# A third expert with a fixed place: three of its weight loads move ahead of the wait for the sorted experts

## The chip, the cores and the metric

One core of a Trainium2 chip runs the whole program as one launch. The metric is the device time in microseconds of that launch. The runs before the change took 867.78, 868.07 and 868.67 us; 868.07 is their median.

## The reference

Two residual layers on 256 tokens of width 1024, all in float32, then a last RMSNorm. Each layer is an attention mixer (layer 0: sparse attention beside block attention; layer 1: latent attention beside a sliding window) and then a mixture of experts. The change is in the mixture:

```
aff    = sigmoid(h @ router_w)                       # 256 x 16
g      = the group of 4 experts whose two best (aff + router_b) sum highest
expert = the 2 best experts of that group, w = aff of them / their sum
for each expert e, on the tokens that chose it:
    y = (silu(x @ w_gate[e]) * (x @ w_up[e])) @ w_down[e]
out[token] += w * y
```

There are 16 experts with `w_gate` and `w_up` of 1024 x 512 and `w_down` of 512 x 1024, 6 MB for one expert and 96 MB for a layer. All of them are read, whatever the router chooses; only the number of tokens on each differs.

## The kernel before

**Places and groups.** An expert's tokens are worked on in a *place*, a fixed number of 32-token blocks. `GROUPS` (L31) lists seven groups of places, four blocks (128 tokens) in each; a pair (p, n) is place p with n blocks. Which expert sits in which place is settled at run time: `places()` (L1357) ranks the first `SORTED` experts by their number of tokens, and place p gets the expert whose rank is `RANKS[p]`. The experts behind `SORTED` keep the place of their own number. Before, 14 experts are sorted, and experts 14 and 15 keep places 14 and 15, which are group 0. So group 0's weights can be requested before the router has run (`load_both`, L1179); all other groups need the sorted numbers, which VectorE writes into `ex_p` (L1378).

**A group** (class `Group`, L1211) does this: `__init__` reads the numbers of its experts from `ex_p` into registers of the engine that will request the weights (`load_value`, L1348, recorded at L1349). That engine is SP, for group 3 POOL. The read waits for `ex_p`, and everything behind it in that engine's queue waits too. `hidden` requests gate and up (`load_experts`, L1161, its requests at L1171): two tiles of 1 MB for each expert and matrix, h = 0 and 1 with four of the eight k rows each, all experts' first halves before the second halves. Then `gate_up` (L1096) runs the matmuls, one after the other over k, and in each k over the blocks (`parts`, from `blocks`, L1087: two blocks of 64 tokens for a group [2, 2], else four of 32). `rows` (L1272) requests the down weights if need be and runs the down matmuls; `combine` (L1140) adds the result to X.

**Order.** The loop at L1464 handles group i's `hidden`, then group i-1's `rows`, so the requests in SP's queue go: gate and up of group 0, then the wait for `ex_p`, gate and up of group 1, down of group 0, gate and up of group 2, down of group 1, and so on. Before group 3, SP requests group 2's down weights and comes to `rest()` (L1445). That is a chain of branches (L1453) for tokens that overflow their place: `rounds()` (L1386) has counted how many extra rounds of 64 tokens are needed, and none is run where nothing overflows. PE, ACT, DVE and SP take the branch; SP waits there for all its outstanding loads. POOL requests group 3's weights on its own queue and doesn't branch.

**Tiles.** Weights go through 15 tiles of 1 MB, 10 named `slot` and 5 named `room`, handed on as they are freed by the matmuls that read them (`slot`, L139). The same tiles carry the mixers' weights and the adaLN weights (`ada_load`, L250). Ahead of group 0 in a layer's expert stage stand two adaLN chunks, two tiles each.

The scheduler orders each engine's instructions by their place in the program and puts in the waits; SP's requests stand in its queue in the order in which they are written.

Of the kernel before, what the change touches and what calls it, by code (L numbers as in the profile page):

```python
# [17 lines left out]
ET = mybir.EngineType  # L18
# [4 lines left out]
NE, DE = 16, 512  # L23
# [4 lines left out]
RING, EXTRA = 10, 5  # L28


GROUPS = [[(14, 2), (15, 2)], [(0, 3), (1, 1)], [(2, 2), (3, 1), (4, 1)], [(5, 2), (6, 2)], [(7, 2), (8, 1), (9, 1)],  # L31
          [(10, 2), (11, 2)], [(12, 2), (13, 2)]]
RANKS = 0, 9, 1, 10, 11, 2, 3, 4, 12, 13, 5, 6, 7, 8
SORTED = len(RANKS)
BLOCK = 32


def shape_constants():
# [40 lines left out]
    iota = np.tile(1000 + np.arange(96, dtype=f)[None], (P, 1))  # L79
    ranks = np.tile(np.array(RANKS, f)[None], (P, 1))  # L80
    places = sorted(x for g in GROUPS for x in g)
    size = np.tile(np.array([BLOCK * n for _, n in places], f)[None], (P, 1))

    owner = np.concatenate([np.repeat(np.eye(len(g), dtype=f), [BLOCK * n for _, n in g], axis=0) for g in GROUPS], axis=1)
    rank = np.tile((4 - np.arange(4)).astype(f)[None], (P, 1))
# [22 lines left out]
def trunk(ctx, tc, ins, out):  # L108
    nc = tc.nc
    mm, vec, act, pool, sp = nc.tensor.matmul, nc.vector, nc.scalar, nc.gpsimd, nc.sync  # L110
# [14 lines left out]
    def bank(tag, shape, name=None):  # L125
        t = ps.tile([P, 512], F32, tag=tag, name=name or tag)
        n = 1
        for s in shape[1:]:
            n *= s
        v = t[:shape[0], :n]  # L130
        if len(shape) == 3:
            v = v.rearrange("p (a b) -> p a b", b=shape[2])
        elif len(shape) == 4:
            v = v.rearrange("p (a b c) -> p a b c", b=shape[2], c=shape[3])
        return v
# [3 lines left out]
    def slot(n_k, n):  # L139

        tag = order.pop(0)
        order.append(tag)
        t = room() if tag == "wx" else ring.tile([P, 2048], F32, tag="w", name="slot")
        return t[:, :n_k * n].rearrange("p (k f) -> p k f", k=n_k)

    def room():

        return rooms.tile([P, 2048], F32, tag="wx", name="room")
# [91 lines left out]
    def const(name):  # L240
        i, a, n = _WHERE[name]
        return KT[i][:, a:a + n]
# [7 lines left out]
    def ada_load(layer, n):  # L250
        return load_k8(ins["ada_w"][layer][:, n * 512:(n + 1) * 512])
# [69 lines left out]

    def ada_chunk(layer, c, W):


        v, half = divmod(c, 2)
        if half == 0 and v in (2, 5):
            GATE[v] = big.tile([P, D], F32, name="GATE", tag="GATE")
            pool.dma_start(GATE[v], ins["ada_b"][layer:layer + 1, v * D:(v + 1) * D].to_broadcast([P, D]))
        b = bank("tp", [P, 512])
        for k in range(8):  # L330
            g = (k % 4) * 32
            mm(b[g:g + 32], csil[:, k, 1 - half:33 - half], W[k], start=k < 4, stop=k >= 4)  # L332
            if k == 3:
                yield
        if half == 0:
            halves.append(ada_tile())
        t = halves[0]
        o, i = t, b
        if v not in (2, 5):
            o, i = t.rearrange("p (k m) -> p m k", k=8), b.rearrange("p (m k) -> p m k", k=8)  # L340
        if half == 0:
            act.copy(o, i)
            return
        vec.tensor_tensor(o, o, i, ALU.add)
        yield
        ada_end(layer, v, halves.pop())

    def fill(n=1):
        for _ in range(n):
            if fills:  # L350
                layer, c = fills.pop(0)
                W = first.pop(0) if first else ada_load(layer, c)
                for _ in ada_chunk(layer, c, W):
                    pass

    def ada_steps(n, rest):

        todo = [fills.pop(0) for _ in range(n)]
        W = ada_load(*todo[0])
        yield  # L360
        for i, at in enumerate(todo):
            ahead = ada_load(*todo[i + 1]) if i + 1 < n else None
            for _ in range(rest):
                yield
            yield from ada_chunk(*at, W)
            W = ahead
# [99 lines left out]
    def features(x, k=8):  # L466

        return x.rearrange("p (m k) -> p m k", k=k)

    def by_k(x, k=8):  # L470

        return x.rearrange("p (k m) -> p m k", k=k)
# [494 lines left out]
    def moe(cp, wk, layer, norm, end):  # L967
# [106 lines left out]
        def flush():  # L1074
            while late:
                late.pop(0)()

        def in_line():

            last = [None]  # L1080

            def add(*args, **kw):
                with tc.issue_after(last[0].ins) if last[0] else nullcontext():
                    last[0] = mm(*args, **kw)  # L1084
            return add

        def blocks(group):  # L1087


            ns = [n for _, n in group]  # L1090
            if ns == [2, 2]:
                return [(1, slice(64, 128)), (0, slice(0, 64))]
            at = [a for a, n in enumerate(ns) for _ in range(n)]
            return [(at[j], slice(BLOCK * j, BLOCK * j + BLOCK)) for j in reversed(range(4))]

        def gate_up(XG, c0, parts, Wg, Wu):  # L1096

            out = []
            for W, tag in ((Wg, "mm"), (Wu, "sc")):
                b = bank(tag, [P, 512])  # L1100
                put = in_line()
                for k in range(8):
                    for a, at in parts:
                        put(b[at], XG[:, k, c0 + at.start:c0 + at.stop], W[a][k], start=k == 0, stop=k == 7)
                out.append(b)
                flush()
            g, u = out
            hid = wk.tile([P, 512], F32, tag="hid", name="hid", bufs=1)
            hq = wk.tile([P, 512], F32, tag="hq", name="hq", bufs=1)
            act.activation(hid, g, AF.Silu)  # L1110
            vec.tensor_tensor(by_k(hq, 4), features(u, 4), features(hid, 4), ALU.mult)  # L1111
            return hq
# [66 lines left out]
        def load_both(nm, e0):  # L1179

            v = ins[nm][layer][e0:e0 + 2].rearrange("a (p k) f -> p a k f", k=8)
            tiles = []
            for k in range(0, 8, 2):
                t = slot(4, 512).rearrange("p (a k) f -> p a k f", a=2)
                sp.dma_start(t, v[:, :, k:k + 2, :])
                tiles.append(t)
            return [Rows([(t[:, a], 2) for t in tiles]) for a in range(2)]

        def pick_tile():
            return wk.tile([P, 2, 256], F32R, tag="pick", name="pick")  # L1190

        def picked(groups, pos):

            o = pick_tile()
            places, at = [x for g in groups for x in GROUPS[g]], 0
            while places:
# [9 lines left out]
        def gathered(o, n):  # L1206
            XG = hp.tile([P, 8, n], F32, tag="HT", name="XG")
            gather(XG, n, o)
            return o, XG

        class Group:  # L1211


            def __init__(self, i, o, XG, c0):
                self.first, self.last = i == 0, (layer, i) == (1, len(GROUPS) - 1)
                self.after = i == 3
                self.o, self.XG, self.c0 = o, XG, c0
                self.p0, self.n = GROUPS[i][0][0], len(GROUPS[i])
                self.parts = blocks(GROUPS[i])
                first = sum(len(g) for g in GROUPS[:i])  # L1220
                self.owner = const("owner")[:, first:first + self.n]
                es = list(range(self.p0, self.p0 + self.n))
                if i:
                    es = [load_value(ex_p[:, e:e + 1], [(ET.SP, ET.Pool)[self.after]], NE - 1) for e in es]
                self.es = es
                self.Wd = None

            def hidden(self):
                names = ("moe_w_gate", "moe_w_up")
                if self.first:  # L1230
                    W = [load_both(nm, self.p0) for nm in names]
                else:
                    W = [load_experts(nm, self.es, 8, queue=(sp, pool)[self.after], fine=self.last and nm == names[1])
                         for nm in names]
                self.hid = gate_up(self.XG, self.c0, self.parts, *W)

            def slots(self):
                self.OT = wk.tile([P, 2, P], F32R, tag="OT", name="OT")
# [109 lines left out]
        def load_value(at, engines, top):  # L1348
            _, v = nc.values_load_multi_w_load_instructions(  # L1349
                at, engines=engines, min_val=0, max_val=top, skip_runtime_bounds_check_because="sums of indicators")  # L1350
            return v[0]


        ex_p = cp.tile([1, 16], I32, name="ex_p")
# [103 lines left out]
        o, XG = gathered(*picked([0], route[:, 0:2]))  # L1458
# [5 lines left out]
        for i in range(len(GROUPS)):  # L1464
            p = Group(i, o, XG, 128 * (i > 0 and i % 2 == 0))
# [11 lines left out]
            if i % 2 == 0 and i < 5:  # L1477
                o, XG = gathered(*then)
# [299 lines left out]
```

## Time and profile before

| | |
|---|---|
| median of 3 runs | 868.07 us (867.78 to 868.67) |
| profiled execution | 869.42 us |
| its span, first to last instruction | 867.2 us |
| TensorE busy | 746.6 us, 86% of the span |
| VectorE, ScalarE, GpSimd busy | 377.8, 237.4, 115.6 us |
| mean granted TensorE clock | 0.932 |
| read from HBM | 289.16 MB, 335 GB/s over the span |

PE is TensorE's matmul row, DVE VectorE, ACT ScalarE, POOL GpSimd, SP the engine that issues most loads; a q behind a name (SPq, PEq) is the engine's sequencer, which waits, branches and issues. A busy share over the whole span is a mean over stages with different limits: the mixers of attention and the expert stages of the two layers have to be read apart.

### The profile page before, as it was taken

The numbers are of one execution on the slowest core, as the hardware profiler recorded it, in microseconds if no ns is written. First come the engines' busy times: TensorE is split into PE (matmuls) and PEld (weight loads), VectorE is DVE, ScalarE is ACT, GpSimd is POOL, SyncE is SP. The second block draws the span as 40 slices with busy tenths as digits, with TensorE's granted clock in tenths as the row PEclk, the third lists the DMA queues.
The fourth block names the chain that finished last, engine by engine and source line by source line (L and its number), as shares of the span: only waits on it lengthen the run. The fifth ranks groups of instructions, "written<-read, shape, count | busy, mean of one in ns | idle before, by whom it ended". The sixth has DMA issues, their size and how long they took to land. (4 is left out here: it accounts for less than half of the span.)

```text
span 867.2 us, 12251 instructions
## 1 busy us (share of the span) xinstructions
PE 746.6 (86%) x4499; PEld 381.9 (44%) x4499; DVE 377.8 (44%) x1091; ACT 237.4 (27%) x569; POOL 115.6 (13%) x118
## 2 busy tenths in 40 slices
PE   4699999999799969759997899979899967769996
PEld 1298765557443332214332568556443322214233
DVE  2285777767831231103206654876912031103214
ACT  1254545545311010001112454545111010002012
POOL 2020111233100001000011223344000001000001
PEclk9699999999699999879999999988699988979998
DMA  9999878796299998999999997733499989999992
GB/s 328 349 328 387 321 248 217 280 376 219 96 422 418 419 417 337 419 420 419 419 415 389 360 350 196 288 130 122 179 419 419 419 361 395 420 420 419 416 396 77
DMA packets 84840, 291.14 MB, mean 336 GB/s; under 512 B 9174, under 2 KB 23202, under 8 KB 63010
## 3 DMA queue, kind: packets, MB, share of 16 engines
q1 hardware_dynamic: 76976, 258.36, 77.9%
q0 software_dynamic: 4608, 29.37, 8.3%
q10 hardware_dynamic: 3186, 2.51, 0.9%
q8 instruction: 39, 0.64, 0.3%
q14 instruction: 31, 0.25, 0.1%
HBM read 289.16 MB, written 1.06 MB: 335 GB/s over the span
## 5 line engine op out<-in xcount | busy, mean ns | idle before, releaser
L1084 PE MATMUL o<-slot,hT 128*32 128x512 f32 (+2 forms) x448 | 93.5, 619 | 14.0 <-PEq L1453 13.1
L1084 PE MATMUL sc<-slot,XG 128*64 128x512 f32 (+1 forms) x416 | 92.1, 646 | 13.6 <-DMA slot<-in_moe_w_up_dram 13.6
L1111 DVE TENSOR_TENSOR hq<-sc,hid 128x512 f32<-128x512 f32 x14 | 14.7, 1049 | 184.3 <-PE sc L1084 184.3
L1084 PE MATMUL mm<-slot,XG 128*32 128x512 f32 (+1 forms) x416 | 85.9, 624 | 5.2 <-DMA slot<-in_moe_w_gate_dram 5.2
L507 ACT CAST hl<-slot 128x512 fp32r<-128x512 f32 (+2 forms) x112 | 60.7, 557 | 72.8 <-PE mm L524 45.8
L464 POOL TENSOR_TENSOR hl<-slot,hl 128x512 fp32r<-128x512 f32 x40 | 53.2, 1333 | 163.1 <-ACT hl L507 135.7
L1084 PE MATMUL mm<-room,XG 128*64 128x512 f32 (+1 forms) x224 | 57.1, 629 | 5.6 <-DMA room<-in_moe_w_gate_dram 5.6
L1084 PE MATMUL o<-room,hT 128*32 128x512 f32 (+2 forms) x208 | 58.6, 603 | 2.0 <-DMA room<-in_moe_w_down_dram 2.0
L1155 DVE SCALAR_TENSOR_TENSOR adac<-o,w,GATE 128x512 f32<-128x512 f32 (+1 forms) x29 | 21.2, 732 | 82.5 <-PE o L1084 81.5
L522 PE MATMUL mm<-HH,hl 128*128 128x256 f32 x176 | 54.5, 311 | 2.3 <-ACT HH L496 2.3
L1084 PEld LDWEIGHTS sc<-slot,XG 128*64 128x64 f32 (+1 forms) x416 | 25.3, 132 | 70.1 <-issue 48.6
L1137 ACT CAST yg<-adac 128x512 fp32r<-128x512 f32 (+1 forms) x28 | 17.1, 612 | 140.0 <-DVE adac L1155 140.0
L332 PE MATMUL tp<-slot,csil 128*32 128x512 f32 x344 | 49.2, 648 | 4.4 <-DMA slot<-in_ada_w_dram 4.2
L1084 PE MATMUL sc<-room,XG 128*32 128x512 f32 (+1 forms) x224 | 45.0, 656 | 8.3 <-DMA room<-in_moe_w_up_dram 8.3
L1068 ACT ACTIVATE XG<-tp,mod,mod 128x256 f32<-128x256 f32 (+1 forms) x32 | 17.2, 538 | 124.0 <-PE tp L1066 124.0
L524 PE MATMUL mm<-HH,hl 128*128 128x256 f32 x176 | 50.0, 286 | 0.6 <-DVE hl L464 0.6
L523 PE MATMUL mm<-HH,hl 128*128 128x256 f32 x176 | 50.4, 287 | 0.1
L1084 PEld LDWEIGHTS o<-slot,hT 128*32 128x32 f32 (+1 forms) x448 | 25.5, 125 | 54.3 <-issue 36.0
L464 DVE TENSOR_TENSOR hl<-slot,hl 128x512 fp32r<-128x512 f32 (+2 forms) x72 | 42.6, 611 | 15.3 <-ACT hl L507 15.0
L1066 PE MATMUL tp<-pick,XH 128*128 128x256 f32 (+1 forms) x128 | 41.9, 347 | 4.0 <-DVE XG L1070 2.6
L1145 DVE TENSOR_TENSOR X<-X,tp 128x512 f32<-128x512 f32 (+1 forms) x56 | 36.0, 675 | 16.5 <-PE tp L1144 16.2
L1144 PE MATMUL tp<-yg,OT 128*128 128x512 f32 (+1 forms) x112 | 36.6, 431 | 7.5 <-ACT yg L1137 3.5
(377 smaller groups left out, 1305.9 us busy)
## 6 DMA issues: line engine op xcount, KB each, us to landing
slot<-in_ada_w_dram SPq DMA_DIRECT2D x43, 1024.0 KB, 10.3
slot<-in_moe_w_gate_dram SPq DMA_DIRECT2D x37, 1024.0 KB, 15.1
slot<-in_moe_w_down_dram SPq DMA_DIRECT2D x35, 1024.0 KB, 19.7
slot<-in_moe_w_up_dram SPq DMA_DIRECT2D x34, 1024.0 KB, 18.6
room<-in_moe_w_up_dram SPq DMA_DIRECT2D x20, 1024.0 KB, 16.8
room<-in_moe_w_gate_dram SPq DMA_DIRECT2D x19, 1024.0 KB, 15.2
room<-in_moe_w_down_dram SPq DMA_DIRECT2D x17, 1024.0 KB, 18.8
slot<-in_ev_w_in_dram SPq DMA_DIRECT2D x8, 1024.0 KB, 9.5
```

Of the source, the lines that this page charges most:

```text
L332: mm(b[g:g + 32], csil[:, k, 1 - half:33 - half], W[k], start=k < 4, stop=k >= 4)
L464: eng.tensor_tensor(lo, v, hi.bitcast(F32), ALU.subtract)
L507: act.copy(hi, src)
L522: mm(o, a[0], b[0], start=start, stop=False, skip_group_check=True)
L523: mm(o, a[0], b[1], start=False, stop=False, skip_group_check=True)
L524: mm(o, a[1], b[0], start=False, stop=stop, skip_group_check=True)
L1066: mm(b, xk[i][:, t, k, :], o[:, t, 0:n], start=t == i == 0, stop=t == i == 1)
L1068: act.activation(XG[:, k, :], b, AF.Identity, bias=sh[:, k:k + 1], scale=fa[:, k:k + 1])
L1084: last[0] = mm(*args, **kw)
L1144: mm(cb, OT[:, t, :], x, start=i == 0, stop=i == 1)
L1145: vec.tensor_tensor(X[:, t, sl], X[:, t, sl], cb, ALU.add)
L1155: vec.scalar_tensor_tensor(v, y, w, gate[:, sl], ALU.mult, ALU.mult)
```

## The change

Three experts keep their place instead of two. Experts 14 and 15 stay in group 0; expert 13 keeps place 13 in group 1, beside the sorted place 12. The table of groups is written anew, so that group 1 is [2, 2] and group 3 is [3, 1]; `SORTED` falls from 14 to 13. In group 1 the blocks are taken in the other order, and the requests are made by a function of its own, `load_mixed`: both halves of expert 13's gate and the first half of its up, then the read of place 12's expert from `ex_p`, then that expert's gate, the second half of expert 13's up, and the sorted expert's up.

```diff
-GROUPS = [[(14, 2), (15, 2)], [(0, 3), (1, 1)], [(2, 2), (3, 1), (4, 1)], [(5, 2), (6, 2)], [(7, 2), (8, 1), (9, 1)],
-          [(10, 2), (11, 2)], [(12, 2), (13, 2)]]
-RANKS = 0, 9, 1, 10, 11, 2, 3, 4, 12, 13, 5, 6, 7, 8
+GROUPS = [[(14, 2), (15, 2)], [(12, 2), (13, 2)], [(0, 2), (1, 1), (2, 1)], [(3, 3), (4, 1)], [(5, 2), (6, 1), (7, 1)],
+          [(8, 2), (9, 2)], [(10, 2), (11, 2)]]
+RANKS = 1, 8, 9, 0, 10, 2, 11, 12, 3, 4, 5, 6, 7
...
-                if i:
+
+                self.mixed = i == 1
+                if self.mixed:
+                    self.parts = self.parts[::-1]
+                elif i:
                     es = [load_value(ex_p[:, e:e + 1], [(ET.SP, ET.Pool)[self.after]], NE - 1) for e in es]
...
                 if self.first:
                     W = [load_both(nm, self.p0) for nm in names]
+                elif self.mixed:
+                    W = self.load_mixed(*names)
...
+            def load_mixed(self, gate_, up):
+
+                e1 = self.es[1]
+
+                def half(nm, e, h):
+                    t = slot(4, 512)
+                    sp.dma_start(t, ins[nm][layer][bass.ds(e, 1)].rearrange("o (p k) f -> p (o k) f", k=8)[:, 4 * h:4 * h + 4, :])
+                    return t, 4
+                g1, u1 = [half(gate_, e1, 0), half(gate_, e1, 1)], [half(up, e1, 0)]
+                e0 = self.es[0] = load_value(ex_p[:, self.p0:self.p0 + 1], [ET.SP], NE - 1)
+                g0 = [half(gate_, e0, h) for h in range(2)]
+                u1.append(half(up, e1, 1))
+                u0 = [half(up, e0, h) for h in range(2)]
+                return [Rows(g0), Rows(g1)], [Rows(u0), Rows(u1)]
```

## Rows read from the trace of the kernel before

**Rows 1.** The page: GB/s that the DMA moved, in 40 equal slices.
```profile
GB/s 328 349 328 387 321 248 217 280 376 219 96 422 418 419 417 337 419 420 419 419 415 389 360 350 196 288 130 122 179 419 419 419 361 395 420 420 419 416 396 77
```

**Rows 2.** Stretches: us, busy PE, PEld, DVE, ACT, POOL, clock, DMA share, GB/s.
```profile
212.00:232.00 20.00, 14.44 (x89) 9.06 (x87) 14.89 (x58) 8.62 (x11) 6.23 (x2) 0.78 0.07 27
...
602.00:618.00 16.00, 12.13 (x61) 6.04 (x60) 12.90 (x48) 7.31 (x9) 5.95 (x2) 0.72 0.00 1
...
778.00:867.00 89.00, 77.08 (x398) 30.45 (x394) 28.06 (x52) 16.46 (x37) 3.89 (x4) 0.97 0.83 331
```

**Rows 3.** SP's waits (us, times, longest): 200:233, then 586:618, then 300:330.
```profile
SPq L1349 <- DVE ex_p L1378: 21.6, 1, 21.6
SPq L1349 <- PE mm L524: 6.9, 1, 6.9
...
SPq L1349 <- DVE ex_p L1378: 29.3, 1, 29.3
...
SPq L1453 <- SPq L1453: 27.0, 7, 5.3
```

**Rows 4.** Timeline of SP in layer 0: start us, us, request, count.
```profile
201.10 1.58 SPq L1185 DMA_DIRECT2D slot<-in_moe_w_up_dram  x2
231.94 1.91 SPq L1171 DMA_DIRECT2D slot<-in_moe_w_gate_dram  x3
234.09 0.41 SPq L1171 DMA_DIRECT2D room<-in_moe_w_gate_dram  x1
...
235.31 4.22 SPq L1171 DMA_DIRECT2D slot<-in_moe_w_up_dram  x3
...
262.57 3.82 SPq L1171 DMA_DIRECT2D slot<-in_moe_w_gate_dram  x3
...
300.85 0.33 SPq L1171 DMA_DIRECT2D room<-in_moe_w_down_dram  x1
329.38 7.72 SPq L1171 DMA_DIRECT2D room<-in_moe_w_gate_dram  x2
```

**Rows 5.** DMA 240:320, then the loads of 617.98, 251.99, 300.85: last, us to landing.
```profile
DMA packets 4597, 33.54 MB, mean 419 GB/s; under 512 B 507, under 2 KB 507, under 8 KB 507
...
slot<-in_moe_w_gate_dram SPq DMA_DIRECT2D x1, 1024.0 KB, 4.9
...
slot<-in_moe_w_gate_dram SPq DMA_DIRECT2D x1, 1024.0 KB, 21.2
...
room<-in_moe_w_down_dram SPq DMA_DIRECT2D x1, 1024.0 KB, 27.7
```

**Rows 6.** PE's waits (us, times, longest): 232:320, then 320:470, then 704:867.
```profile
PE o L1084 <- DMA room<-in_moe_w_down_dram: 0.9, 1, 0.9
...
PE sc L1084 <- DMA room<-in_moe_w_up_dram: 8.3, 1, 8.3
PE o L1084 <- PEq L1453: 6.8, 1, 6.8
PE mm L1084 <- DMA slot<-in_moe_w_gate_dram: 5.2, 1, 5.2
PE sc L1084 <- DMA slot<-in_moe_w_up_dram: 3.0, 2, 1.8
...
PE sc L1084 <- DMA slot<-in_moe_w_up_dram: 10.6, 3, 6.7
...
PE mm L1084 <- DMA room<-in_moe_w_gate_dram: 5.6, 2, 4.3
```

**Rows 7.** Timeline of PE: group 1's gate (second half) and up (both halves).
```profile
262.38 0.59 PE L1084 MATMUL mm<-room,XG 128*32 128x512 f32 x1
...
265.81 0.59 PE L1084 MATMUL sc<-slot,XG 128*32 128x512 f32 x1
...
269.24 3.62 PE L1084 MATMUL sc<-slot,XG 128*32 128x512 f32 x32
```

**Rows 8.** Timeline of DVE: the first of the sort's wide operations.
```profile
228.18 0.35 DVE L1369 TENSOR_TENSOR adac<-key 128x196 f32<-128x196 f32 x1
```

## The prediction, made before the changed kernel ran

> **What bounds the kernel now.** I read the page first, then the stretches around the two expert stages, then who waits there. The page's 40 slices of GB/s [rows 1] are what the reader is to see first: long runs at about 420, twice broken by a hole (the low values in the middle) in which attention and routing run, and then 420 again until the kernel is nearly over. 420 is the ceiling that this kernel reaches; the two expert stages live under it. The holes end in near-silence: from 212 to 232 us the DMA moves 27 GB/s, from 602 to 618 us 1 GB/s [rows 2]. SP's own waits say why [rows 3]: in layer 0 it waits 21.6 us, in layer 1 29.3 us, at L1349 for `ex_p` (L1378), the sorted experts. Every load of group 1 stands behind that read in SP's queue. SP's last load before the wait goes out at 201.10 (two of them, over by 202.68), the next at 231.94 [rows 4].
>
> Once the wait ends, loads follow one another at 419 GB/s [rows 5], 1,048,576 bytes in 2.50 us; that is the price of a 1 MB tile whenever the stream is full. The first one lands 4.9 us after its issue [rows 5], so 2.4 us of start-up come before 2.5 us of data; in a full stream the 2.4 us lie behind the load ahead.
>
> Two things stand in the way of simply saying "the stage is as long as its bytes". From 232 to 320 us TensorE waits for a load only once, 0.9 us [rows 6]: it is itself nearly full there, and data come well ahead (a load issued at 251.99 takes 21.2 us to land, so several stand in line [rows 5]). And at the branch of `rest()` (L1453) the queue drains. Behind the branch TensorE waits for loads 8.3 + 5.2 + 3.0 = 16.5 us in layer 0, and 10.6 + 5.6 = 16.2 us in layer 1 [rows 6]. So the load stream, not TensorE, decides when the stage ends, and TensorE has 16 us in hand in each layer.
>
> **The change part by part.**
> *Moved ahead of the wait:* expert 13's gate and up come in four loads of 1 MB; three of them (two of gate, one of up) now stand ahead of the read of `ex_p`. SP reaches them at 202.68. One wait that SP has there, 6.9 us for the last output-projection matmul [rows 3], may come before them: then they start at 209.6. Three loads: 2.4 + 7.5 = 9.9 us, landed by 219.5 at the latest. The wait ends at 231.94, so the silent stretch covers them with 12 us left; in layer 1 it is 29.3 us long. Cost 0; if the cover were gone they would cost their 7.5 us again, and nothing would be won. Nothing else is queued on SP behind them before the read of `ex_p`, and ACT's, POOL's and PE's queues are not touched. What they take off the stream behind the wait is 3 x 2.50 = 7.5 us per layer.
>
> *Buffers:* weights live in 15 tiles that are handed on as they come free. Four hold adaLN chunks, eight hold group 0; three are free. That is just what the early loads need: before, the first three behind the wait go out in 1.91 us, and the fourth at once too [rows 4]. But the hand-on order changes further down. Group 2's fourth to sixth gate loads take the next tiles that group 1 frees. Before, these were two gate tiles freed together as TensorE begins the second half of group 1's gate (262.38) and one more at 265.81 [rows 7]; SP's issue at 262.57 follows within 0.2 us [rows 4]. Now, in order of request, they are expert 13's gate tiles (free at 262.4 and 265.8) and its first up tile (269.24 [rows 7]). The load ahead of them lands at 251.99 + 21.2 = 273.2 before, 265.7 now. Fourth: issued 262.6, data could start at 265.0, no loss. Fifth: issued 266.0, data from 268.4 where the stream is free at 268.2, 0.2 lost. Sixth: 269.4, data from 271.8 against 270.9, 0.9 lost. So 1.1 of the 7.5 us go back: the lead is 6.4 us. TensorE wants these tiles only when groups 0 and 1 are through, and the 0.9 us are its one wait for a load up to 320 [rows 6]. Bounds of this term: 0 lost, or all three wait for group 1's last up tile at about 272.8: then the sixth lands at 272.9 + 2.4 + 7.5 = 282.8, later than before, and the lead is gone there. I take 1.1, since SP's issues follow TensorE's rows so closely.
>
> *The branch:* SP leaves it when its last load has landed, 300.85 + 27.7 = 328.55; the next goes out at 329.38 [rows 4, 5]. The drain is 27.0 us of waits, the jump's own 5.3 us (the longest of the seven) hidden under it [rows 3]. With a lead of 6.4 us SP leaves at 322.1. TensorE's stall of 6.8 us at the same branch [rows 6] hangs on no load, so it stays. Restart gap before: data again from 329.38 + 2.4 = 331.8, after 328.55: 3.2 us without data. I leave it as it is; it could shrink to 0 (POOL's loads for group 3 may still be in flight then), or grow by TensorE's 0.9.
>
> *Behind the branch:* POOL's last five loads of group 3 and SP's first of group 4 need only SP's exit, 6 x 2.5 = 15 us of stream; I take it as full as before, 6.4 us earlier. TensorE's 16.5 and 16.2 us of waits there are each more than that. What is late next is the same load stream. It carries to the end of the stage: in layer 0 the next layer's weights stand in the same queue, so layer 1 begins 6.4 us earlier as a whole; in layer 1 the last stretch is TensorE's (77.08 busy of 89 us [rows 2]), and it begins when the up weights of group 4 land.
>
> *Groups and sort:* 14 groups of matmuls before and after, as many of either shape (four groups with two blocks of 64, three with four of 32), so TensorE's work is the same. The sort goes over 13 instead of 14: five operations of about 0.35 us on 196 elements [rows 8] lead to `ex_p`, now on 169. At most 5 x 0.35 x 27/196 = 0.24 us per layer, at least 0; I take 0.1.
>
> *Overflow rounds:* counting the reference's router on its own inputs, no place overflows in either layer in either table (fullest expert 58 and 71 tokens on a place of 96; expert 13 has 26 and 23 on 64). So `rest()` runs nothing before or after.
>
> **The sum.** 2 x (7.5 - 1.1 + 0.1) = 13.0 us. Against the profiled execution's own time (869.42, with a span of 867.2) that gives 856.4; it lies 1.35 above the median of the runs shown, 868.07, so I forecast 855.1 for that.
>
> [...] The trace has 419 GB/s over 80 us [rows 5]. [...]
>
> **The rivals.**
> *Buffers in a worse order (lead halved).* If the scheduler hands the tiles on later than I worked out, 3 to 4 us per layer remain: 868.07 - 2 x 3.5 = 861. For: SP issues within 0.2 us of TensorE's release, so it does wait for buffers there. Against: loads in line cover 15 us and more.
> *TensorE is the bound (gain gone).* Only the 0.9 us in front of the branch is won: 868.07 - 2 x 0.9 = 866.3 or more. For: TensorE is nearly full from 232 on. Against: its 16 us of waits behind the branch.
> *A stall like the jump's.* At the branch TensorE stands 6.8 us that no load ends, with the DMA full [rows 6]. If the routing met one such stall per layer, because weights now move beside it, 6.8 - 6.5 would be left: 868.07 + 0.6, no change. Against: the three loads are over before the sort begins. [...]
> *Slower: the third early load finds no buffer.* It would stand in front of the read of `ex_p` until group 0's first gate tile is free, which is when SP's load of 239.2 goes out (the last of the three from 235.31 to 239.53 [rows 4]). The first load behind the wait would go out at about 240.2 instead of 231.94: 8.3 lost against 7.5 won and 1.1 lost again, 2 x 1.9: 871.9. It decides from the moment that fewer than three tiles are free. Against: four loads went out in 2.6 us behind the wait.
> *More: the restart gap closes too.* 2 x 3.2 on top: 848.7. For: POOL's loads run on beside SP's drain. Against: POOL's fourth waits for SP's exit too.
>
> **How the numbers follow.** Forecast 0.67 (851.5 to 858.5); halved lead 0.14; TensorE 0.05; stall 0.02; slower 0.05; gap closes 0.07. What the measurement can tell from no change is about 1.7 us (0.2%). Faster: 0.67 + 0.14 + 0.07 and a part of the TensorE case, 0.89. Slower 0.05, same 0.06. The range goes from 850, half of the last rival outside, to 862.5, which takes in most of the halved lead; outside lie about 0.18.
>
> **What would show it.** In the SP timeline three loads of expert weights before 215 us and before 605 us, and five instead of eight between the wait and group 0's down loads. GB/s in 212 to 232 up by at most 3 MB. SP's first load behind the branch near 323 instead of 329.4. TensorE's load waits behind the branch smaller by about 6 us per layer; both stages shorter by the same. I am wrong if the first load behind `ex_p` comes later than 1 us after the cast of `ex_p`, if the branch is left at 328 as before, or if TensorE's waits behind it shrink while the stage doesn't.

## The result, and the profile after

The changed kernel took 857.44 us (median of four runs, 857.31, 857.58, 859.34 and 854.84), the kernel before beside it 867.92: ratio 0.9876 [0.9849, 0.9903], 10.5 us less. The profiled run took 857.31 us with a span of 855.6; the rows below are from it.

The page's line for GB/s [rows 1]:
```profile
GB/s 326 347 321 385 325 274 201 260 400 294 136 423 364 419 419 339 419 421 418 419 418 391 357 363 185 262 203 270 116 419 381 418 346 412 420 418 419 416 398 89
```
The hole is shallower near its end in both layers (294 and 136 where 219 and 96 stood, 203 and 270 where 130 and 122 did). But two dents are new: 364 in slice 13 and 381 in slice 31, just where the stream before ran at 420.

Stretches of the changed kernel, columns as in [rows 2]; the last two are the 36 us around the *hand-on* of buffers, in which TensorE reads group 1's tiles for the last time and SP loads group 2's weights into them; they ran at 418 and 419 GB/s before:
```profile
212.00:232.00 20.00, 14.46 (x90) 9.09 (x89) 14.83 (x58) 8.62 (x11) 6.20 (x2) 0.80 0.38 156
602.00:618.00 16.00, 12.19 (x65) 7.18 (x59) 15.52 (x67) 3.89 (x8) 1.26 (x1) 0.82 0.25 92
...
246.00:282.00 36.00, 35.29 (x178) 15.03 (x173) 6.96 (x19) 4.68 (x10) 0.00 (x0) 1.00 0.96 387
628.00:664.00 36.00, 35.29 (x180) 15.34 (x176) 8.24 (x22) 5.91 (x11) 0.00 (x0) 1.00 0.99 396
```
The silent stretch of layer 0 carries 2.6 MB more (20 us x 129 GB/s). A full stream has 420, so 387 over 36 us are 36 x 33/420 = 2.8 us without data, and 396 are 2.1 us. In layer 0 all of it lies where group 2's fourth to sixth gate load are asked for:
```profile
262.00:276.00 14.00, 14.00 (x68) 4.86 (x68) 1.06 (x1) 1.16 (x2) 0.00 (x0) 1.00 0.88 336
```
14 us at 336 GB/s are 2.8 us without data. That is what the hand-on took back.

SP's timeline in layer 0 [rows 4]:
```profile
203.21 0.99 SPq L1249 DMA_DIRECT2D slot<-in_moe_w_gate_dram  x2
206.58 0.33 SPq L1249 DMA_DIRECT2D slot<-in_moe_w_up_dram  x1
232.29 0.96 SPq L1249 DMA_DIRECT2D room<-in_moe_w_gate_dram  x2
...
264.10 6.36 SPq L1171 DMA_DIRECT2D slot<-in_moe_w_gate_dram  x3
...
324.61 12.51 SPq L1171 DMA_DIRECT2D room<-in_moe_w_gate_dram  x2
```
Three loads go out ahead of the read. Group 2's fourth to sixth gate load (264.10, 267.5, 270.1) go out later than before (262.6, 263.1, 266.1), and behind the branch SP starts 4.8 us earlier (329.38 before; the branch, L1453 before, is L1474 now).

PE's waits [rows 6], 320:470 and then 704:856:
```profile
PE sc L1084 <- DMA room<-in_moe_w_up_dram: 9.7, 1, 9.7
PE o L1084 <- PEq L1474: 5.2, 1, 5.2
PE mm L1084 <- DMA slot<-in_moe_w_gate_dram: 3.1, 2, 2.8
...
PE sc L1084 <- DMA slot<-in_moe_w_up_dram: 1.6, 1, 1.6
PE o L1084 <- DMA room<-in_moe_w_down_dram: 1.0, 1, 1.0
...
PE sc L1084 <- DMA slot<-in_moe_w_up_dram: 9.9, 2, 8.5
PE mm L1084 <- DMA room<-in_moe_w_gate_dram: 5.4, 1, 5.4
```
The waits for loads behind the branch add up to 15.4 us in layer 0 and 15.3 in layer 1. The 15.4 hold a wait of 1.0 us for a down load; before, there was such a wait too, and the prediction's 16.5 leave it out:
```profile
PE o L1084 <- DMA room<-in_moe_w_down_dram: 1.1, 1, 1.1
```
Like for like, then, 17.6 us became 15.4 in layer 0 and 16.2 became 15.3 in layer 1: 2.2 and 0.9 us less, and yet the kernel is 10.5 us faster.

### The profile page after: what moved, and what is told of

Read it like the earlier page. It is cut to its first block, busy times and chain, and to the rows that moved or that the text cites. A ratio compares the mean times of both kernels' runs of the same rounds, so it can differ in the third digit from the quotient of the medians.

```text
span 855.6 us, 12225 instructions
## 1 busy us (share of the span) xinstructions
PE 745.3 (87%) x4499; PEld 384.6 (45%) x4499; DVE 377.7 (44%) x1095; ACT 237.3 (28%) x569; POOL 114.5 (13%) x118
## 5 line engine op out<-in xcount | busy, mean ns | idle before, releaser
L1084 PE MATMUL o<-slot,hT 128*32 128x512 f32 (+2 forms) x464 | 96.3, 621 | 8.7 <-PEq L1474 8.7
L1084 PE MATMUL sc<-slot,XG 128*32 128x512 f32 (+1 forms) x464 | 91.9, 612 | 11.5 <-DMA slot<-in_moe_w_up_dram 11.5
L1084 PE MATMUL mm<-room,XG 128*32 128x512 f32 (+1 forms) x288 | 65.8, 612 | 5.4 <-DMA room<-in_moe_w_gate_dram 5.4
L1084 PE MATMUL o<-room,hT 128*64 128x512 f32 (+2 forms) x192 | 59.7, 598 | 1.0 <-DMA room<-in_moe_w_down_dram 1.0
L1084 PEld LDWEIGHTS sc<-slot,XG 128*32 128x32 f32 (+1 forms) x464 | 26.6, 125 | 61.2 <-issue 47.8
L1084 PE MATMUL sc<-room,XG 128*32 128x512 f32 (+1 forms) x176 | 39.7, 647 | 9.7 <-DMA room<-in_moe_w_up_dram 9.7
## 6 DMA issues: line engine op xcount, KB each, us to landing
slot<-in_moe_w_down_dram SPq DMA_DIRECT2D x35, 1024.0 KB, 15.3
```

## The experiments

**The same instructions again, and TensorE's blocks turned round.** The first run repeats the changed kernel. The second takes its block order back:
```
 if self.mixed:
-    self.parts = self.parts[::-1]
+    pass
```


> The changed kernel again, as the level for the runs beside it. All theories: 857.4 us, between 854.8 and 859.3 as its first four runs lay, some 10.5 us under the kernel before.

> TensorE reads expert 13's block ahead of expert 12's in group 1, where the changed kernel reads them the other way round. Theory (the hand-on loses 2.7 and 1.9 us a layer since expert 13's buffers, first in the line, come free late): they come free about 1 us earlier, the 4th load behind them starts near 263 instead of 264.1 us in the first layer, and about 1 us a layer comes back: 855.4 us. Rival (TensorE waits for expert 12's tiles either way, so that both blocks end together): 857.4 us, unchanged. Other side: the two blocks' out-of-step order shifts to the up weights and costs as much there, 858 to 859 us.

Measured: 854.93 us, ratio 0.9854 [0.9835, 0.9873], and 856.24 us, 0.9873 [0.9855, 0.9890] (before: 867.49). The blocks' order makes no difference in the time that can be told; the streams through the hand-on are 394 and 386 GB/s in the one, 397 and 395 in the other, 5.1 and 4.1 us without data. So the order is not the main cause of the loss. It has a small part in it: with the blocks turned back, group 2's fourth load goes out 7.09 us after TensorE begins group 1's gate (254.94 to 262.03), in the changed kernel 7.95 us after (256.15 to 264.10); the sixth goes out some 14 us after in both.

**Two misses: loads moved in the text alone.** The requests were written behind the read of `ex_p`, all three in one kernel, the up load in the other:
```
-g1, u1 = [half(gate_, e1, 0), half(gate_, e1, 1)], [half(up, e1, 0)]
 e0 = self.es[0] = load_value(ex_p[:, self.p0:self.p0 + 1], [ET.SP], NE - 1)
+g1, u1 = [half(gate_, e1, 0), half(gate_, e1, 1)], [half(up, e1, 0)]
```


> The new grouping and the new order of the loads stay, but all three loads of expert 13 stand behind the read of the sorted experts. Theory (the whole gain is the three loads' early start): their lead of 7.5 us a layer is gone and with it the loss at the hand-on of buffers, so the time of the kernel before, 868 us, within 1.5 us. Rival (the new grouping helps by itself, by its narrower sort, by the order of TensorE's two blocks or by another order of buffers): part of the 10.5 us stays, 862 to 865 us.

> Only the two gate loads of expert 13 are requested ahead of the read; the up load stands behind it. Theory (the third load's lead is spent where buffers are handed on, since expert 13's first gate buffer comes free at 264 us in the first layer and no earlier): the lead is 5.0 us a layer, the buffers are then needed 2.5 us later than with three and little is lost at them (0.2 us where three lost 2.7 us), so 4.8 and 5.0 us a layer are left where three leave 4.7 and about 5.9: 858 us, within 1 us of the changed kernel. Rival (the gain goes by the bytes requested early): two thirds of 10.5 us, so 861 us.

Measured: 854.97 and 855.47 us, ratios 0.9858 [0.9833, 0.9883] and 0.9851 [0.9831, 0.9871]. Taken at its word the first would have refuted the theory. Its SP timeline says otherwise:
```profile
203.21 0.99 SPq L1249 DMA_DIRECT2D slot<-in_moe_w_gate_dram  x2
206.80 0.33 SPq L1249 DMA_DIRECT2D slot<-in_moe_w_up_dram  x1
231.91 0.95 SPq L1249 DMA_DIRECT2D room<-in_moe_w_gate_dram  x2
```
The loads still stand ahead of the read: the scheduler has put requests that could go in front of a read that couldn't yet. In both kernels SP's requests come in the changed kernel's order, and the traces hold as many instructions, so both count as the changed kernel once more. (The statement ahead of the prediction, that SP's requests stand in its queue as they are written, is thus not true of requests written behind a read that waits.) What they give is a measure of scatter: one program, four medians of 854.9 to 857.4 us. Differences under some 2.5 us aren't told apart here.

**None, one, two and four loads ahead.** Now an order on SP's instructions holds the loads (none ahead; the others likewise); for four, the second up half goes ahead too:
```
+read, (e0,) = nc.values_load_multi_w_load_instructions(ex_p[...], engines=[ET.SP], ...)
+with tc.issue_after(read[0].ins): g1, u1 = [half(gate_, e1, 0), half(gate_, e1, 1)], [half(up, e1, 0)]
```


> All three loads of expert 13 are held behind the read of the sorted experts, by an order put on SP's instructions; all else is as in the changed kernel (855.1 us in the last round of runs, the mean of three runs of the same instructions; the kernel before 867.5). Theory (the gain is the early start of the three loads, less what the hand-on takes back): 867.5 us, 866 to 869. Rival (the new grouping alone helps): 862 to 865 us.

> One load of expert 13, its first gate half, ahead of the read, two behind. Theory (each 1 MB load ahead gives a lead of 2.5 us a layer, as long as the hand-on of buffers takes none of it back, which it did to 1.9 to 2.7 us of 7.5 with three): 2.5 us in each of two layers, 862.5 us. Rival (by bytes, a third of 12.4 us): 863.4 us. The two agree here; what would speak against both is a step (867 or 856 us).

> Both gate loads of expert 13 ahead of the read, the up load behind it, now held there by an order on SP's instructions. Theory (the third load's lead is spent where buffers are handed on): 5.0 us in each layer with 0.2 us lost, so 858 us at most; against three ahead the third load is then worth 2 to 3 us at most over both layers. Rival (by bytes, two thirds of 12.4 us): 859.3 us.

> A fourth load ahead of the read: the second up half of expert 13 too, into a buffer of the other pool. Theory (buffers handed on by TensorE at group 1 already hold back group 2's loads with three ahead): the fourth lead is lost there in whole, 855 us, within 1 us of three ahead. Rival (by bytes, each load ahead 2.5 us a layer, as long as its buffer is free): 850 us. Other side: its buffer isn't free before the read, so that SP waits for it with the sorted loads queued behind: 856 to 862 us.

Measured (before: 867.96): 867.30, ratio 0.9994 [0.9975, 1.0013]; 862.94, 0.9938 [0.9917, 0.9958]; 857.31, 0.9871 [0.9851, 0.9892]; 857.19, 0.9877 [0.9857, 0.9897]. Without the early start the change is worth nothing that can be measured: grouping, sort and block order together bring 0.7 us. The first load ahead brings 4.4 us and the second 5.6, about the 2 x 2.5 us that each is priced at. The third and the fourth bring nothing beyond the scatter. The fourth found its buffer, at 218.26, long before the read. The same two stretches, none ahead, then two, then four:
```profile
246.00:282.00 36.00, 34.56 (x174) 15.29 (x170) 8.04 (x22) 5.90 (x11) 0.00 (x0) 1.00 1.01 419
628.00:664.00 36.00, 35.28 (x174) 14.52 (x170) 6.15 (x17) 4.40 (x8) 0.00 (x0) 1.00 1.01 420
```
```profile
246.00:282.00 36.00, 35.01 (x176) 15.07 (x172) 7.66 (x21) 4.98 (x10) 0.00 (x0) 1.00 1.00 409
628.00:664.00 36.00, 35.29 (x178) 15.21 (x174) 7.17 (x19) 4.67 (x9) 0.00 (x0) 1.00 1.00 413
```
```profile
246.00:282.00 36.00, 34.56 (x174) 15.15 (x171) 7.70 (x21) 5.91 (x11) 0.00 (x0) 1.00 0.96 387
628.00:664.00 36.00, 35.30 (x180) 15.02 (x176) 10.28 (x25) 5.91 (x11) 0.00 (x0) 1.00 0.92 370
```
TensorE's busy time hardly moves (34.6 to 35.3 of 36 us), the stream's rate does. With none ahead SP asks for group 2's fourth load at 262.08, 31.0 us after the first load behind the read; with two at 263.38, 32.0 after; in the changed kernel 31.8 after. Counted from the moment at which TensorE begins group 1's gate (254.14, 255.47, 256.15) it is 7.91 to 7.95 us in all three. The buffers come free when TensorE gets there, whatever lies ahead of the read; each load ahead only shortens the line of loads that hides that.

**TensorE made busier ahead of the hand-on.** Group 0's up gets ten matmuls more:
```
-for k in range(8):
+for n, k in enumerate([*range(extra), *range(8)]):   # extra = 5 for group 0's up, else 0
```


> The changed kernel, with ten matmuls more (five of the eight k rows of group 0's up weights are multiplied a first time, and their sums are then overwritten): 5 pairs of 0.43 us, 2.2 us more of TensorE in each layer, ahead of group 1's gate. Theory (with three loads ahead it is TensorE's own work up to group 1's gate that sets when buffers come free for group 2's fourth to sixth load, so the lead is spent there to the last us): 2.2 us a layer lost, 4.3 us, so about 861 us, 7 us under the kernel before instead of 11. Rival (what holds the loads there is the stream itself or the wait for the sorted experts, and TensorE has room): unchanged, 857 us, 11 us under before.

Measured: 866.71 us, ratio 0.9981 [0.9967, 0.9995]; 1.4 us under before (868.07) instead of 11. The direction is the theory's; its size was wrong, since a pair of these matmuls takes 0.86 us and not 0.43. TensorE's timeline of group 0's up:
```profile
242.97 3.60 PE L1084 MATMUL sc<-room,XG 128*64 128x512 f32 x16
246.41 1.02 PE L1084 MATMUL sc<-slot,XG 128*64 128x512 f32 x4
247.27 3.60 PE L1084 MATMUL sc<-room,XG 128*64 128x512 f32 x16
```
From 242.97 to 247.27 the five extra pairs took 4.30 us, not 2.2: 8.6 us over two layers, 9 to 11 were lost. In the two stretches the stream fell to 348 and 322 GB/s, 6.2 and 8.4 us without data. So TensorE's work there is paid in full once the loads are ahead. What the same ten matmuls would cost the kernel before was not run. An estimate from its rows: its fourth load went out at 262.57 and the load ahead of it landed at 273.2, so the load could go out 8.2 us later (up to 273.2 - 2.4) without a gap in the stream, and 4.3 us would cost the stream nothing. In layer 1 the trace of this run also has some of TensorE's matmuls in another order than the changed kernel, from group 1 to behind the branch, so the excess over 8.6 us, up to 2.6, isn't explained.

**Group 0's down weights ahead instead, and its rows too.** Group 0's experts are known, so its down weights could always have gone ahead of the read. On the kernel before:
```
 p.hidden()
+if i == 0: p.load_down()          # both kernels
 if before is not None:
     before.rows()                 # second kernel: for i == 1 ahead of p.hidden()
```


> The kernel before, its grouping kept (two experts in place), with one edit: the four down loads of group 0, whose experts are known, are requested ahead of the read of the sorted experts instead of behind group 1's gate and up. Theory: the lead is the same as with four loads of expert 13 (10 us at most), but the buffers of these loads are given back only when TensorE has multiplied group 0's down, part of it behind group 1's gate and up, so group 2's loads wait longer: more than half of the lead is lost, 860 to 866 us. Rival (the lead counts by its bytes, whichever weights it holds): 848 to 852 us.

> As the run with group 0's down loads ahead, and TensorE multiplies group 0's down ahead of group 1's gate. Theory (the hand-on by TensorE is what spends the lead): the four buffers come free near 262 to 264 us instead of one each at 263.5, 266.9 and 269.6 us, so less of the lead is lost: 5.5 to 7.5 us a layer are left of 10, so 853 to 857 us, at or below the changed kernel. Rival (the lead is capped elsewhere, near 5.3 us a layer, whatever is ahead): 857 us. Other side: group 1's gate comes 3.6 us later on TensorE, and the loads that take its buffers wait for that: 860 us.

Measured (before: 868.07): 866.43, ratio 0.9984 [0.9969, 0.9999]; and 852.67, 0.9821 [0.9799, 0.9842], below both kernels. These four loads ahead alone win almost nothing; with group 0's down multiplied ahead of group 1's gate, so that TensorE gives their buffers back early, they pay. (That order of TensorE's without the loads ahead was not run. In the kernel before the stream is full through this stretch, at 418 and 419 GB/s, so it has no gap there to close.) SP's timeline and TensorE's of the second:
```profile
202.82 3.82 SPq L1171 DMA_DIRECT2D slot<-in_moe_w_down_dram  x3
217.59 0.33 SPq L1171 DMA_DIRECT2D room<-in_moe_w_down_dram  x1
231.32 0.35 SPq L1171 DMA_DIRECT2D room<-in_moe_w_gate_dram  x1
...
261.60 3.78 SPq L1171 DMA_DIRECT2D slot<-in_moe_w_gate_dram  x3
```
```profile
254.04 1.08 PE L1084 MATMUL o<-slot,hT 128*64 128x512 f32 x4
...
264.94 0.62 PE L1084 MATMUL mm<-slot,XG 128*32 128x512 f32 x1
```
Group 0's down runs from 254.04, group 1's gate only at 264.94. The fourth to sixth load of group 2 go out within 3.8 us from 261.60, where the changed kernel takes 6.4 us from 264.10:
```profile
246.00:282.00 36.00, 35.28 (x240) 14.33 (x236) 9.98 (x20) 5.05 (x9) 0.00 (x0) 1.00 0.99 404
628.00:664.00 36.00, 35.29 (x252) 14.42 (x252) 10.70 (x22) 6.01 (x11) 0.00 (x0) 1.00 0.98 400
```
The kernels so far in one table. Lead: 2 layers x 2.5 us x loads ahead. Lost: 36 x (420 - GB/s)/420 over the two stretches. Measured: median of before less that of the kernel.

```
loads ahead                GB/s       lead   lost   left   measured
none                       419, 420    0      0.1   -0.1    0.7
one                        419, 420    5.0    0.1    4.9    5.0
two                        409, 413   10.0    1.5    8.5   10.7
three (the change)         387, 396   15.0    4.9   10.1   10.5
three, again               394, 386   15.0    5.1    9.9   12.6
three, blocks turned back  397, 395   15.0    4.1   10.9   11.3
four                       387, 370   20.0    7.1   12.9   10.8
three, TensorE busier      348, 322   15.0   14.6    0.4    1.4
down of group 0            320, 338   20.0   15.6    4.4    1.6
down and rows of group 0   404, 400   20.0    3.1   16.9   15.4
```
The two misses, the changed kernel once more, have 396 and 387 GB/s and 395 and 395, which leaves 10.1 and 10.7 us; 12.5 and 12.0 were measured. Two terms, the price of a load and the stream's rate, give every time within 3 us. That is too coarse to tell what the third and the fourth load bring, and enough to tell 1.4 and 1.6 us from 10 and 15.

**Two loads less ahead of the branch.** On the last kernel:
```
-out[i].append((t, n))
+out[i].append(out[i][0] if less and h and i else (t, n))   # group 2's down; the load is left out
```


> As the run with group 0's down loads and rows ahead (852.7 us, 15.4 us under the kernel before), but two of the six down loads of group 2, the last that SP requests ahead of the branch, are left out in each layer (the second halves of two experts' down weights; their first halves are multiplied in their place). What it asks: what sets the length of TensorE's stall behind the branch, 3.4 to 6.9 us in the traces so far. Theory (the stall ends later where the weight stream is still moving when TensorE comes to the branch): the stream dries up 5 us earlier, before or as TensorE gets there; the stall falls from 6.2 and 6.1 us to 3.4 to 4 us in the two layers, SP's first load behind the branch comes 2 to 3 us earlier, and the time falls by 4 to 6 us, to 847 to 849 us. Rival (the stall has one length wherever TensorE comes to the branch with this program): 6.2 us as before, 852.7 us, within 1 us, since the stream stood still at the branch anyway.

Measured: 841.61 us, ratio 0.9708 [0.9681, 0.9736]. Neither theory came true (847 to 849 and 852.7 us): by the ratios 868 x (0.9821 - 0.9708) = 9.8 us fewer, four loads of 2.5 us. The bytes count in full, though the stream breaks off at the branch (271 and 260 GB/s over TensorE's stalls in the two layers, where a full stream has 420). On the stall it doesn't decide: TensorE came to the branch earlier as well, so the stream was moving in both layers. Its stalls, layer 0 and layer 1:
```profile
PE o L1084 <- PEq L1453: 4.3, 1, 4.3
...
PE o L1084 <- PEq L1453: 6.3, 1, 6.3
```

## Why the prediction was right, and where it was not

- **The cause: right.** The load stream decides, and the early start alone brings the gain: none ahead 867.3, two ahead 857.3.
- **The early loads cost nothing: right.** 203.21 to 206.91, with the read's first load at 232.29 (before 231.94).
- **Each is worth 2.50 us a layer: right for two, not for the third.** It carries a lead past the read (issued at 206.58), and most of it is lost at the hand-on, near 264 us: 857.31 us with two ahead, 854.9 to 857.4 with three.
- **The hand-on, -1.1: mis-sized, 2.8 and 2.1.** This is the term of the sum that was wrong in size: "Fourth: issued 262.6, data could start at 265.0, no loss. Fifth: [...] 0.2 lost. Sixth: [...] 0.9 lost." The order of the buffers was right, the issues came at 264.1, 267.5 and 270.1, 1.5, 1.5 and 0.7 us later than written. 0.6 us of each is that TensorE begins group 1's gate later in this trace; before, then after:
```profile
255.55 1.07 PE L1084 MATMUL mm<-slot,XG 128*32 128x512 f32 x8
```
```profile
256.15 1.07 PE L1084 MATMUL mm<-room,XG 128*64 128x512 f32 x2
```
  The other 0.9 us of the first two is the turned blocks: expert 13's block now comes behind place 12's in each k, and its gate tiles are let go later (the fourth load goes out 7.95 us after the gate's begin, 7.02 before and 7.09 with the blocks turned back). The prediction took the times at which TensorE lets go from the kernel before as they stood, and gave the block order no price. The rest is arithmetic: a load lands 4.9 us after its issue or 2.5 us behind the one ahead, whichever is later. From the third's landing at 265.9 this gives 269.0, 272.4 and 275.0 (the trace has 274.9), 1.6 us behind a full stream. The rate of 336 GB/s puts all 2.8 us between 262 and 276 us; the 1.2 us by which it exceeds the arithmetic I can't assign. "Loads in line cover 15 us and more", which I held against the halved lead, was true of the kernel before; the change itself uses up that line. When the fourth load was asked for, the loads ahead of it had 10.6 us to go before (262.57 to 273.2), and 1.8 us after (264.10 to 265.9).
- **The sort, +0.1:** not seen by itself. With none ahead the whole rest of the change is worth 0.5 us by the ratio, between -1.1 and 2.2 by its interval.
- **SP behind the branch, "near 323":** 324.61. Its last load of 297.83 took 25.9 us to land, at 323.7; the rule was right, and the 1.7 us are as much as the hand-on took beyond the 1.1.
- **TensorE's stall "stays": wrong,** 6.8 to 5.2 and 6.2 to 3.5 us (below).
- **TensorE's waits behind the branch "smaller by about 6 us": wrong.** They fell by 2.2 us in layer 0 and 0.9 in layer 1. TensorE left the branch at 324.48 (before 324.90), and its last wait for group 4's up ended 5 us earlier; before, then after:
```profile
385.57 0.62 PE L1084 MATMUL sc<-slot,XG 128*32 128x512 f32 x2 [1.25 <-DMA slot<-in_moe_w_up_dram]
```
```profile
380.60 0.62 PE L1084 MATMUL sc<-slot,XG 128*32 128x512 f32 x2 [1.63 <-DMA slot<-in_moe_w_up_dram]
```
  Between these points TensorE was busy 2.6 us less and idle 1.9 us less. From 345 to 365 us its granted clock was 1.00, where it had been 0.83 before (0.50 from 349.6 to 356.3 us, 1.00 ahead of that and behind it). In that stretch it had stood 5.2 us for a gate load before, up to 352.63, and its next matmuls took 1.03 us each; now it stood 2.8 us, up to 348.18, and they took 0.59. The stage follows the stream; TensorE's time in it is partly waiting and, before, partly running at a granted clock of 0.50, so the sum of its waits, the "16 us in hand" of the prediction, isn't its slack.
- **The sum:** 13.0 forecast, 15.0 less 4.9 by the rows, 10.5 and 12.6 measured. The rivals with TensorE as the bound, with a stall at the routing, without a buffer for the third load and with a closed restart gap fell; the halved lead was the nearest, with the right place: it put the loss at 4 us a layer, the forecast at 1.1, and 2.8 and 2.1 were measured. So the forecast was right on the cause. Its gain lies 2.5 us above the measured 10.5, about what the hand-on took beyond the 1.1 in the two layers (2.7 us), though the scatter between the repeats is as large. The wrong steps on TensorE's stall and its waits didn't change the sum, which was made from the stream.

## What to carry to other kernels

A transfer moved ahead of a wait is worth its bytes only as far as the next place where buffers are handed on (here 15.0 us by the bytes, 10.5 and 12.6 measured): look there how long the line of queued loads is, and take the times at which the engine lets go from the order that it will have after the change. Two moves that look alike can differ by all of the gain: group 0's four down loads ahead won 1.6 us where their buffers came back late and 15.4 where the engine's order gave them back first. And before an experiment that moves a request is believed, its timeline has to show that the request moved.

## What was not expected of the hardware

TensorE's stall at the branch, which no load ends, isn't constant. It was longest where weights moved all through it and shortest where the stream dried up as TensorE arrived. Stretches of such stalls, columns as in [rows 2]: the kernel before, layer 0; the changed kernel, layer 1, then layer 0; the kernel with rows ahead, layer 0.
```profile
318.10:324.90 6.80, 0.00 (x0) 0.03 (x1) 0.85 (x2) 0.00 (x0) 0.00 (x0) 0.80 1.01 412
```
```profile
701.00:704.50 3.50, 0.00 (x0) 0.00 (x0) 0.84 (x3) 0.00 (x0) 0.00 (x0) 1.00 0.23 89
319.30:324.50 5.20, 0.02 (x4) 0.05 (x5) 0.89 (x3) 0.00 (x0) 0.00 (x0) 0.86 0.52 213
```
```profile
314.80:321.00 6.20, 0.00 (x0) 0.00 (x0) 0.84 (x3) 0.00 (x0) 0.00 (x0) 0.72 0.62 254
```
3.5 us at 89 GB/s, 5.2 at 213, 6.2 at 254, 6.8 at 412; but the last experiment has 4.3 us at 271 GB/s in layer 0 and 6.3 at 260 in layer 1, so the rate alone doesn't set it. In each of the four stalls of the kernel before and of the changed kernel the trace has one packet of 16 KB on a queue that the page lists as `q8 instruction`, and TensorE's first matmul follows the end of that packet by 1.7 to 1.8 us. What varies most is when the packet starts: 0.8 us after TensorE fell idle in the stall of 3.5 us (701.78 to 702.84, TensorE again at 704.54), 2.3 after in that of 5.2 us (321.62 to 322.64, TensorE at 324.48), 3.4 after in the 6.2 us that the kernel before has in layer 1 (707.43 to 708.50, TensorE at 710.22), 4.0 after in that of 6.8 us (322.08 to 323.16, TensorE at 324.90). The start of that packet thus goes with the stall's length in these four. That TensorE waits for it is inferred from this regularity alone, and why it starts early or late stays open: no run here varies it alone.
